# Four pairs as seven products in every gate-up group from the third on, and another order at the end of each group

## The chip, the cores and the metric

The kernel runs on one core of one Trainium2 chip. The metric is the device time of one execution in microseconds. Five engines work side by side, each with its own queue of instructions: PE (TensorE, matmuls; its weight loads are listed as PEld), DVE (VectorE), ACT (ScalarE), POOL (GpSimd) and SP (SyncE, which only issues DMAs here). They wait for each other through semaphores.

## What is computed

One layer of an encoder in float32, 256 tokens of width 2048: a feed-forward block (FFN), a mixer (a gated recurrence beside windowed attention), a second FFN. The change lies in the first half of each FFN, the gate-up product:

```
ff = swiglu(rms_norm(x, pre_norm_ffn1), w_ffn1_gate_up, w_ffn1_down)

def swiglu(x, w_gate_up, w_down):
    gate, up = jnp.split(x @ w_gate_up, 2, axis=-1)      # 2048 -> 2 x 5632
    return (jax.nn.silu(gate) * up) @ w_down
```

The result must have nearly float32 accuracy.

## The kernel before

**Three products for one.** TensorE multiplies numbers of a shortened float32 format (fp32r). Each operand is split into a high part and the rest: ACT casts the high part (L176, `scalar.copy`), DVE or POOL subtracts it from the original for the low part (L177, `tensor_tensor`). A product is then three matmuls: high times high, high times low, low times high (`three`, L438). All of them are issued at one line, L447, with 128 x 128 weights (activations) and 512 moving columns.

**Groups and pairs.** The 5632 gate and 5632 up columns are worked off in 11 groups (`NG`) of 512 gate and 512 up columns. Within a group the 2048 rows of the weight are 8 pairs (u = 0 to 7) of two blocks of 128 rows. One pair of one group is a tile `raw` of 128 x 2048: four blocks b11, b12, b22, b21 of 512 columns, 1 MB, fetched by two DMAs from SP (`fetch_tile`, L140). There are five such tiles; a tile is refilled (`load_next`, L970) as soon as its last split is issued. Four PSUM banks c[m][n] hold the sums, m a half of the tokens, n gate or up.

**Plain or seven.** A *plain* pair is 8 block products of three matmuls: 24. A pair done as a *seven* uses the 2 x 2 scheme with seven products: 21 matmuls. It needs sums of the weight blocks and sums of the activations, and four more banks p = P1, P5, P6, P7, which collect over all sevens of a group and are added into c once, at the group's end. The seven products of `products` (L473) are numbered 0 to 6: P1; into c00; into c01; P5; P7; P6; into c10. For a seven, `prepare` (L979) splits block b11 and has POOL issue a DMA that adds the neighbouring blocks in memory onto the tile (`add_second`, L146, 512 KB). `splits` (L994) then makes three splits of 1024 columns (called lower, upper and last) with two DVE additions of 512 columns between (L1001, L1002). A plain pair needs two splits of 1024 only. The splits go into rings of five high and five low tiles.

**Which pairs are sevens.** `MIXED_IN` is (2, 4, 5, 6), `FIVE` is (2, 3, 4, 5, 6). Group 1 has three sevens, group 2 four, groups 3 to 10 (`FIVE_IN`) five. Group 0 is done by other code. The fifth needs sums of activations for pair 3, which group 2 makes on the side (`sums_apart`, L1129), and one more room for a prepared block (`spare`, L1121).

**Order.** The loop at L1417 is written out by hand (`manual_schedule`), so each engine's instructions stand in program order. For each group 1 to 10: `first_pairs` (pairs 0 and 1, with the last steps of the group before between: its silu, gate times up, transposes, all in `units`, L1170); `pair_ahead` for pairs 2 to 5, which splits one pair ahead and prepares sevens further ahead; then, at L1421, the splits of pair 7 (a plain one, its low parts by POOL), the products of pair 6 (a seven, L1422), and `boundary` (L1252).

**The boundary** brings P1, P5, P6, P7 into the c banks and works pair 7 between. ACT copies P1 to SBUF (L1259). DVE then does eight additions: into c00 (L1260), a + P6 (L1261), + P7 (L1262), into c10 (L1263), a difference with P5 (L1266), into c01 (L1267), another (L1269), into c11 (L1270). Each that writes a bank must come before the matmuls of pair 7 into that bank. Pair 7's matmuls are parted by `take_parted` (L1015): `upper(m, n)` is the four with high weights for one bank, `lower()` the eight with low weights for all. The order on TensorE is upper of c00, c10, c01, c11, then lower. In pair 6 the order of products is 0, 1, 3, 4, 5, 6, 2.

Of the kernel before, what the change touches and what calls it, by code (L numbers as in the profile page):

```python
# [17 lines left out]
ALU = mybir.AluOpType  # L18
# [30 lines left out]
def hymba_layer_kernel(  # L49
# [19 lines left out]
    nc = tc.nc  # L69
# [145 lines left out]
    last = {}  # L215
# [186 lines left out]
    class Blocks:  # L402
# [4 lines left out]
        ahead = None  # L407
# [27 lines left out]
        def bank(self, at):  # L435
            return self.p[at[1]] if at[0] == "p" else self.c[at[1]][at[2]]
# [462 lines left out]
    NG = DFF // 512  # L899
# [5 lines left out]
    ADDED = 3  # L905
    FIVE = (2, 3, 4, 5, 6)
    PREPARED_FIVE = {2: -0.5, 3: 0.5, 4: 1.5, 5: 2.5, 6: 3.5}
    FIVE_IN = range(3, NG)
    AWAY = 8
    MIXED = range(0, 20, 2)  # L910
    MIXED_EARLY = MIXED[:8]
# [11 lines left out]
    class Gated(Blocks):  # L923
# [23 lines left out]
        def plan(self, opened=False):  # L947

            some = MIXED_IN[1:3] if opened else MIXED_IN[:3]
            self.here = {  # L950
                g: FIVE if g in FIVE_IN else MIXED_IN if g > 1 else some for g in range(1, NG)
            }
# [62 lines left out]
        def take_parted(self, g, u):  # L1015

            (h0, l0), (h1, l1) = self.split_of.pop((g, u))
            del self.raws[g, u]
            a = self.tiles[u]

            def parts(m, n, k):
                ms = slice(m * P, (m + 1) * P)
                o = (n ^ k) * 512
                cs = slice(o, o + 512)
                return ("c", m, n), a[:, k, 0, ms], a[:, k, 1, ms], (h0, h1)[k][:, cs], (l0, l1)[k][:, cs]

            def upper(m, n):
                for k in range(2):
                    at, ah, al, h, _ = parts(m, n, k)
                    self.some_of(at, (ah, h), (al, h))  # L1030

            def lower():
                for k in range(2):
                    for n in range(2):
                        for m in range(2):
                            at, ah, _, _, l = parts(m, n, k)
                            self.some_of(at, (ah, l))

            return upper, lower

        def take(self, g, u):

            got = self.split_of.pop((g, u))
            del self.raws[g, u]
            first = self.firsts.pop((g, u), None)
            if first:
                before_fold = u == KT // 2 - 2
                self.products(u, first, *got, (0, 1, 3, 4, 5, 6, 2) if before_fold else range(7))
                return ()
            hs, ls = zip(*got)  # L1050
            return [
                (lambda k=k, m=m, n=n: self.plain(u, hs, ls, m, n, k))
                for k in range(2)
                for m in range(2)
                for n in range(2)
            ]
# [27 lines left out]
    def ffn(gated, w_dn, post_gain, again, gain=None, lead=None, opening=None):  # L1084

        with ExitStack() as st:
# [136 lines left out]
            def some(steps, n):  # L1223
                for _ in range(n):
                    next(steps)

            last = KT // 2 - 1
# [24 lines left out]
            def boundary(g, ahead):  # L1252

                a, b = room_for("z"), room_for("s")
                c, (p1, p5, p6, p7) = gated.c, gated.p
                add = nc.vector.tensor_tensor
                bank, lower = gated.take_parted(g, last)

                nc.scalar.copy(a, p1)  # L1259
                add(c[0][0], c[0][0], a, ALU.add)  # L1260
                add(b, p6, a, ALU.add)  # L1261
                add(a, p7, b, ALU.add)  # L1262
                add(c[1][0], c[1][0], a, ALU.add)  # L1263
                bank(0, 0)
                bank(1, 0)
                add(b, p5, b, ALU.subtract)  # L1266
                add(c[0][1], c[0][1], b, ALU.add)  # L1267
                bank(0, 1)
                add(b, p5, a, ALU.subtract)  # L1269
                add(c[1][1], c[1][1], b, ALU.add)  # L1270
                bank(1, 1)
                lower()
                some(ahead, 2)

            def first_pairs(g, waiting, ahead):

                gated.group(g)
                sevens = FIVE if g in FIVE_IN else MIXED_IN
                if ahead:
                    some(waiting, 2)  # L1280
                    gated.prepare(g, sevens[1], nc.gpsimd)
                    some(ahead, 1)
                else:
                    some(waiting, 1)
                    gated.prepare(g, sevens[1])
                    some(waiting, 1)
                    ahead = gated.splits(g, 1)
                    some(ahead, 2)
                    gated.prepare(g, sevens[2])
                for one in gated.take(g, 0):  # L1290
                    one()
                some(waiting, 1)
                ahead = gated.splits(g, 2)
                some(ahead, 2)
                next(ahead, None)
                some(waiting, 1)
                for one in gated.take(g, 1):
                    one()

            def pair_ahead(g, u):  # L1300

                if u == 2 and g in FIVE_IN:
                    gated.prepare(g, FIVE[3])
                if u == 3:
                    gated.prepare(g, MIXED_IN[3])
                ahead = gated.splits(g, u + 1)
                some(ahead, 2)
                for one in gated.take(g, u):
                    one()
                if u == last - 2 and g < NG - 1:  # L1310
                    gated.prepare(g + 1, MIXED_IN[0])
                for _ in ahead:
                    pass
                if u == last - 2:
                    done = gated.split_of[g, last - 1][-1][1]
                    nc.gpsimd.tensor_copy(warm[:, 2:3], done[:, 0:1].bitcast(F32))
                if g == 1 and u in sums_at:
                    sums_in(sums_at[u])
                if g == 2 and u in (2, 3, 4):
                    if u == 2:  # L1320
                        apart.append(sums_apart(ADDED))
                    next(apart[0])
                if u == 5 and 1 < g <= AWAY // 2 + 1:
                    put_away(2 * g - 4)
                    put_away(2 * g - 3)
# [12 lines left out]
            raws, firsts, got = {}, {}, {}  # L1338
# [73 lines left out]
            with tc.manual_schedule():  # L1412
# [4 lines left out]
                for g in range(1, NG):  # L1417
                    first_pairs(g, waiting, begun)
                    for u in range(2, last - 1):
                        pair_ahead(g, u)  # L1420
                    some(gated.splits(g, last, nc.gpsimd), 2)  # L1421
                    for one in gated.take(g, last - 1):  # L1422
                        one()
                    boundary(g, gated.splits(g + 1, 0) if g < NG - 1 else splits(0))
                    if g < NG - 1:
                        begun = gated.splits(g + 1, 1)
                        next(begun)
                    among = None
                    if g < NG - 1:
                        third = (FIVE if g + 1 in FIVE_IN else MIXED_IN)[2]  # L1430
                        among = lambda g=g, u=third: gated.prepare(g + 1, u, nc.gpsimd)
                    waiting = units(gated.c, rest, among)
                    some(waiting, 2)
# [12 lines left out]
                ahead = splits(1)  # L1446
# [5 lines left out]
                ahead = splits(2)  # L1452
# [4 lines left out]
                for i in range(2, 2 * NU - Pairs.HELD):  # L1457
# [4 lines left out]
                    ahead = splits(i + 1)  # L1462
# [31 lines left out]
    gated = Gated(w_ffn1_gate_up, two_banks())  # L1494
    xt = new_xt()
    gated.see(xt)
    with tc.manual_schedule():
# [17 lines left out]
        first = gated.source(0)  # L1515

        def arrive(i, eng=nc.sync):
# [3 lines left out]
        h, l = (  # L1521
            p.tile([P, 1024], F32R, tag=t, name=nm(t)) for p, t in ((hip, "h"), (lop, "l"))
        )
# [12 lines left out]
        def parts(u, i, n=2):  # L1536

            if i == 0:
                gated.parts[u] = ([], [])
            h, l = (  # L1540
                p.tile([P, 1024], F32R, tag=t, name=nm(t)) for p, t in ((hip, "h"), (lop, "l"))
            )
            w = 1024 // n
            for j in range(n):
                split_act(
                    h[:, j * w : (j + 1) * w],
                    l[:, j * w : (j + 1) * w],
                    raws[u][:, i * 1024 + j * w : i * 1024 + (j + 1) * w],
                )
            for part, of in zip(gated.parts[u], (h, l)):  # L1550
                part.append(of)
# [173 lines left out]
    with ExitStack() as s2:  # L1725
# [142 lines left out]
        with tc.manual_schedule(engines=ordered):  # L1868
            late = [load(mix_tile("N", 6144, kc)) for kc in (2, 3)]
            parts = [split(late[0]), ([], [])]  # L1870
# [35 lines left out]
            bank = spread_begin(ratio, 1)  # L1906
            bounds_ahead()
            first = [split_half(raw, 0)]
# [50 lines left out]
            bank = spread_begin(rest)  # L1959
# [14 lines left out]
            g = mid.tile([P, 2, 512], F32, tag="g", name="g")  # L1974
# [73 lines left out]
        k = wide[:, 0].rearrange("p (d j t) -> p d j t", d=2, t=T)  # L2048
# [342 lines left out]
        g = gates(1)  # L2391
# [27 lines left out]
        gated = Gated(w_ffn2_gate_up, two_banks())  # L2419
# [139 lines left out]
```

## Time and profile before

| | us |
|---|---|
| median of 3 runs (1822.75 to 1824.27) | 1823.04 |
| the profiled execution | 1823.13 |
| its span, first to last instruction | 1821.4 |
| PE busy | 1798.4 |
| DVE busy | 1648.0 |
| ACT busy | 1143.9 |
| POOL busy | 288.5 |

The profile shows one execution. A row of a group of instructions has line, engine, operation, tiles (written <- read) with their shapes, count, then busy time and mean nanoseconds of one, then how long the engine was idle just before them and what ended that. A row of a timeline has start and length in microseconds. A row of the waits says who waited for whom: total, times, longest. PE's busy time is made of instructions that overlap. The first FFN's groups 1 to 10 lie from about 45 to 476 us of the span, the second's from about 1153 to 1587.

### The profile page before, as it was taken

The page shows a single profiled execution, that of the slowest core. Times are in us where ns is not written, and L with a number is a line of the kernel's source. Part 1 is how long each engine was busy: PE and PEld are TensorE (multiplying, and loading weights), DVE is VectorE, ACT ScalarE, POOL GpSimd, SP SyncE. Part 2 cuts the span into 40 slices and gives each one's busy share as a digit, 9 for nine tenths or more (in the row PEclk, how much of TensorE's full clock was granted, in tenths as well). Part 3 has the DMA queues.
Part 4 walks back from the last instruction along what each step waited for, and adds up shares of the span by engine and source line. Part 5 has one row for each costly group of instructions (what it writes and reads, how often), then busy time and mean ns, then how long its engine had stood idle before and what let it go on. Part 6 is the DMA issues. An engine that isn't in the chain of part 4 may idle for free.

```text
span 1821.4 us, 24095 instructions
## 1 busy us (share of the span) xinstructions
PE 1798.4 (99%) x8320; PEld 1480.1 (81%) x8320; DVE 1648.0 (90%) x2154; ACT 1143.9 (63%) x1527; POOL 288.5 (16%) x270
## 2 busy tenths in 40 slices
PE   9999999999999999999999999999999999999998
PEld 7877787777788888888899888877777778788886
DVE  6899999999999999888888888889999999999997
ACT  7556666666665667566667566556666656566663
POOL 0122322222110100000000000022223222200110
PEclk9999999999999999999999999999999999999999
DMA  9789999899799997954555767889999899799895
GB/s 369 231 246 283 284 296 261 262 256 253 237 325 306 310 281 244 295 160 165 181 166 173 254 206 262 249 236 270 285 278 279 255 270 260 199 319 340 270 318 167
DMA packets 130331, 469.05 MB, mean 258 GB/s; under 512 B 14608, under 2 KB 17424, under 8 KB 128672
## 3 DMA queue, kind: packets, MB, share of 16 engines
q1 hardware_dynamic: 109152, 391.18, 59.5%
q0 software_dynamic: 20912, 76.07, 23.5%
q8 instruction: 65, 1.06, 0.2%
q14 instruction: 58, 0.48, 0.1%
q10 hardware_dynamic: 144, 0.26, 0.0%
HBM read 452.77 MB, written 14.68 MB: 257 GB/s over the span
## 4 chain that ended last, share of the span: by engine, by line
PE 86%; DVE 9%; DMA 2%; ACT 1%; issue 1%; SPq 0%; POOL 0%; DVEq 0%; ACTq 0%; POOLq 0%
PE pa L447 39%; PE pb L447 34%; PE pa L315 6%; PE pa L320 3%; DVE l L177 1%; DMA raw<-in_w_ffn_gate_up_dram 1%; ACT h L176 1%; DVE pa L1267 1%; DVE pb L1270 1%; DVE s L1269 1%; DVE z L1262 1%; DVE pb L1263 1%; PE pa L369 1%; DVE s L1261 1%; PE pa L368 1%
## 5 line engine op out<-in xcount | busy, mean ns | idle before, releaser
L176 ACT CAST h<-raw 128x1024 fp32r<-128x1024 f32 (+1 forms) x881 | 850.6, 1002 | 428.2 <-DVE raw L1002 99.8
L177 DVE TENSOR_TENSOR l<-raw,h 128x1024 fp32r<-128x1024 f32 (+1 forms) x789 | 915.6, 1191 | 64.3 <-ACT h L176 45.5
L447 PE MATMUL pa<-h,xt 128*128 128x512 f32 x1214 | 407.9, 393 | 4.3 <-DVE pa L1267 3.9
L447 PE MATMUL pb<-h,xt 128*128 128x512 f32 x1012 | 350.9, 395 | 7.2 <-DVE pb L1270 5.4
L447 PEld LDWEIGHTS pa<-h,xt 128*128 128x128 f32 x1214 | 226.3, 188 | 59.0 <-DVE pa L1267 12.8
L447 PEld LDWEIGHTS pb<-h,xt 128*128 128x128 f32 x1012 | 186.8, 188 | 61.1 <-DVE pb L1270 14.1
L447 PE MATMUL pa<-l,xt 128*128 128x512 f32 x583 | 227.6, 390 | 0.4 <-DVE l L177 0.4
L447 PE MATMUL pb<-l,xt 128*128 128x512 f32 x506 | 197.1, 389 | 0.0
L177 POOL TENSOR_TENSOR l<-raw,h 128x1024 fp32r<-128x1024 f32 (+1 forms) x76 | 142.7, 1897 | 207.7 <-ACT h L176 202.4
L447 PE MATMUL pb<-h,ht 128*128 128x512 f32 x428 | 151.2, 389 | 0.0
L447 PE MATMUL pa<-h,ht 128*128 128x512 f32 x428 | 151.1, 389 | 0.0
L148 POOL DMA_DIRECT2D raw<-in_w_ffn_gate_up_dram x93 | 81.7, 890 | 420.1 <-DVE l L177 369.5
L447 PEld LDWEIGHTS pa<-l,xt 128*128 128x128 f32 x583 | 109.5, 188 | 23.4 <-DVE l L177 1.4
L447 PE MATMUL pa<-h,xs 128*128 128x512 f32 x328 | 117.5, 389 | 0.5 <-DVE sums L399 0.5
L447 PE MATMUL pb<-h,xs 128*128 128x512 f32 x328 | 114.3, 389 | 0.0
L447 PEld LDWEIGHTS pb<-l,xt 128*128 128x128 f32 x506 | 95.0, 188 | 19.8
L315 PE MATMUL pa<-xt,h 128*128 128x512 f32 x448 | 109.9, 393 | 0.0
L315 PEld LDWEIGHTS pa<-xt,h 128*128 128x128 f32 x448 | 81.5, 188 | 15.3
L447 PEld LDWEIGHTS pb<-h,ht 128*128 128x128 f32 x428 | 80.3, 188 | 16.6
L447 PEld LDWEIGHTS pa<-h,ht 128*128 128x128 f32 x428 | 80.3, 188 | 16.6
L148 POOL DMA_DIRECT2D raw<-in_w_ffn_down_dram x42 | 36.5, 868 | 348.0 <-DVE la L177 276.8
L447 PE MATMUL pa<-l,ht 128*128 128x512 f32 x214 | 83.3, 389 | 0.0
(345 smaller groups left out, 2681.5 us busy)
## 6 DMA issues: line engine op xcount, KB each, us to landing
raw<-in_w_ffn_gate_up_dram SPq DMA_DIRECT2D x350, 512.0 KB, 6.4
raw<-in_w_ffn_down_dram SPq DMA_DIRECT2D x176, 512.0 KB, 8.5
raw<-in_w_mix_in_dram SPq DMA_DIRECT2D x94, 512.0 KB, 4.8
raw<-in_w_ffn_gate_up_dram POOLq DMA_DIRECT2D x93, 512.0 KB, 8.9
raw<-in_w_ffn_down_dram POOLq DMA_DIRECT2D x42, 512.0 KB, 8.7
ht<-away SPq DMA_DIRECT2D x24, 512.0 KB, 10.5
raw<-in_w_mix_out_dram SPq DMA_DIRECT2D x24, 512.0 KB, 5.9
away<-ht SPq DMA_DIRECT2D x16, 512.0 KB, 9.2
```

The source lines that it names most:

```text
L148: nc.gpsimd.dma_start(raw[:, 0:1024], src[:, 512:1536], accum_op=ALU.add)
L176: nc.scalar.copy(hi, src)
L177: by.tensor_tensor(lo, src, hi.bitcast(F32), ALU.subtract)
L315: nc.tensor.matmul(slot[f], weights(hs, kk, f), xcol(xt, k), start=(k == 0), stop=(k == KT - 1))
L320: nc.tensor.matmul(slot[f][:, 0:T], weights(ls, kk, f), xcol(xt, kh * 8 + kk, 0), start=False, stop=False,)
L368: nc.tensor.matmul(dst, xh, l[:, o : o + n], start=False, stop=False)
L369: nc.tensor.matmul(dst, xl, h[:, o : o + n], start=False, stop=(k == KT - 1))
L447: nc.tensor.matmul(self.bank(at), lhs, rhs, start=(n == 1), stop=n in (ends, self.of[at]), skip_group_check=n > ends,)
L1261: add(b, p6, a, ALU.add)
L1262: add(a, p7, b, ALU.add)
L1263: add(c[1][0], c[1][0], a, ALU.add)
L1267: add(c[0][1], c[0][1], b, ALU.add)
```

## The change

`FIVE_IN` becomes empty: groups 3 to 10 now take `MIXED_IN`, four sevens (2, 4, 5, 6), like group 2, and pair 3 is plain. The job of `sums_apart` in group 2 and the extra room fall away with it.

The boundary is put in another order. In pair 6 the products go 0, 3, 4, 5, 1, 6, 2 (P1, P5, P7, P6, c00, c10, c01). The splits of pair 7 are issued behind pair 6's products and behind the copy of P1. On DVE a + P6 comes first, then the addition into c00, then as before. Pair 7's matmuls go bank by bank with the low ones of its first block row among them (`most`: 4 + 1), and three low ones of the second block row stand ahead of bank c11. All groups 1 to 10 get this. In `first_pairs` the second split of pair 1 is issued before the preparing of a seven, not behind it.

```
-    FIVE_IN = range(3, NG)
+    FIVE_IN = ()
...
-            def lower():
-                for k in range(2):
-                    for n in range(2):
-                        for m in range(2):
-                            at, ah, _, _, l = parts(m, n, k)
-                            self.some_of(at, (ah, l))
+            def lower(m, n, k):
+                at, ah, _, _, l = parts(m, n, k)
+                self.some_of(at, (ah, l))
...
-                self.products(u, first, *got, (0, 1, 3, 4, 5, 6, 2) if before_fold else range(7))
+                self.products(u, first, *got, (0, 3, 4, 5, 1, 6, 2) if before_fold else range(7))
...
-                bank, lower = gated.take_parted(g, last)
-
                 nc.scalar.copy(a, p1)
+                some(gated.splits(g, last, nc.gpsimd), 2)
+                upper, lower = gated.take_parted(g, last)
+
+                def most(m, n):
+                    upper(m, n)
+                    lower(m, n, 0)
+
+                add(b, p6, a, ALU.add)
                 add(c[0][0], c[0][0], a, ALU.add)
-                add(b, p6, a, ALU.add)
                 add(a, p7, b, ALU.add)
                 add(c[1][0], c[1][0], a, ALU.add)
-                bank(0, 0)
-                bank(1, 0)
+                most(0, 0)
+                most(1, 0)
                 add(b, p5, b, ALU.subtract)
                 add(c[0][1], c[0][1], b, ALU.add)
-                bank(0, 1)
+                most(0, 1)
                 add(b, p5, a, ALU.subtract)
                 add(c[1][1], c[1][1], b, ALU.add)
-                bank(1, 1)
-                lower()
+                for m, n in ((0, 0), (1, 0), (0, 1)):
+                    lower(m, n, 1)
+                most(1, 1)
+                lower(1, 1, 1)
                 some(ahead, 2)
...
                 if ahead:
                     some(waiting, 2)
+                    some(ahead, 1)
                     gated.prepare(g, sevens[1], nc.gpsimd)
-                    some(ahead, 1)
...
-                if g == 2 and u in (2, 3, 4):
+                if FIVE_IN and g == 2 and u in (2, 3, 4):
...
-                    some(gated.splits(g, last, nc.gpsimd), 2)
                     for one in gated.take(g, last - 1):
```

## The prediction

> **What bounds the kernel now.** I read the page first, then the sums over single groups, then the chain of waits, then the timelines of one group's end.
>
> ```profile
> PE 1798.4 (99%) x8320; PEld 1480.1 (81%) x8320; DVE 1648.0 (90%) x2154; ACT 1143.9 (63%) x1527; POOL 288.5 (16%) x270
> L447 PE MATMUL pa<-h,xt 128*128 128x512 f32 x1214 | 407.9, 393 | 4.3 <-DVE pa L1267 3.9
> L447 PE MATMUL pb<-h,xt 128*128 128x512 f32 x1012 | 350.9, 395 | 7.2 <-DVE pb L1270 5.4
> ```
>
> The matmul engine is busy nearly the whole span, so the change is costed on its path: matmuls added, stalls removed. The idle columns name two adds of the group's end (L1267, L1270) but only some 11 us. The next view, waits of the weight loads, gives the same adds and a third a larger figure:
>
> ```profile
> PEld pb L447 <- DVE pb L1270: 14.1, 20, 0.8
> PEld pa L447 <- DVE pa L1267: 12.8, 20, 1.0
> PEld pb L447 <- DVE pb L1263: 10.2, 20, 0.8
> 149.94 2.72 PE pa L447 x12
> ```
>
> Twenty waits each: one in each of the 20 groups that end in `boundary`. The last row is of the chain that ended last: twelve matmuls in 2.72 us, so one costs 0.2267 us when nothing waits. The busy time of one (393 ns) overlaps its neighbours, so stalls must be read from starts. The sums by group, cut at the starts of L1270:
>
> ```profile
> 91.30:134.38 43.08, 42.51 (x189) 34.34 (x188) 39.16 (x52) 26.24 (x34) 10.98 (x9) 1.00 0.83 237
> 134.38:176.81 42.43, 41.90 (x187) 33.83 (x186) 39.76 (x48) 26.74 (x32) 11.86 (x10) 1.00 0.94 275
> 176.81:219.20 42.39, 41.87 (x187) 33.82 (x186) 39.85 (x47) 26.92 (x32) 11.94 (x10) 1.00 0.95 282
> ```
>
> The first row is group 2, which has four pairs as sevens already; the others are groups 3 and 4, with five. So the trace of before shows four beside five at the old end of group. The columns are length, then busy time of PE, PEld, DVE, ACT, POOL, then granted clock (1.00), DMA share and GB/s. Group 2 is longer by 0.65 to 0.69, where three matmuls more (24 for a plain pair, 21 for a seven) make 3 x 0.2267 = 0.68. Vector work, DMA share and rate are lower in it. So a group's length is its matmuls plus something fixed, and neither DVE nor DMA sets it.
>
> The fixed part is at the end of the group. Group 2, TensorE:
>
> ```profile
> 126.41 0.39 PE L447 MATMUL pa<-h,xt 128*128 128x512 f32 x1
> 126.86 0.62 PE L447 MATMUL pa<-h,xt 128*128 128x512 f32 x2
> 129.58 0.39 PE L447 MATMUL pb<-h,xs 128*128 128x512 f32 x1
> 131.17 1.07 PE L447 MATMUL pa<-h,xt 128*128 128x512 f32 x4
> 132.28 1.20 PE L447 MATMUL pb<-h,xt 128*128 128x512 f32 x4
> 133.67 1.19 PE L447 MATMUL pa<-h,xt 128*128 128x512 f32 x4 [0.19 <-DVE pa L1267]
> 135.13 1.20 PE L447 MATMUL pb<-h,xt 128*128 128x512 f32 x4 [0.27 <-DVE pb L1270]
> 136.17 0.39 PE L447 MATMUL pa<-l,xt 128*128 128x512 f32 x1
> ```
>
> Pair 6, a seven, starts at 126.41; 129.58 is the last matmul of its fifth product, P6. Pair 7 starts at 131.17: four matmuls into each of four banks, then eight low ones. From 131.17 to 136.17 there are 16 matmuls, worth 3.63 us, in 5.00: 1.37 us of stall. The bracketed idle times show only 0.46 of it. DVE in the same stretch:
>
> ```profile
> 124.82 2.95 DVE L177 TENSOR_TENSOR l<-raw,h 128x1024 fp32r<-128x1024 f32 x3
> 128.48 0.70 DVE L1260 TENSOR_TENSOR pa<-pa,z 128x512 f32<-128x512 f32 x1 [0.70 <-ACT z L1259]
> 130.00 0.69 DVE L1261 TENSOR_TENSOR s<-pb,z 128x512 f32<-128x512 f32 x1 [0.83 <-PE pb L447]
> 130.73 0.69 DVE L1262 TENSOR_TENSOR z<-pb,s 128x512 f32<-128x512 f32 x1
> 131.53 0.70 DVE L1263 TENSOR_TENSOR pb<-pb,z 128x512 f32<-128x512 f32 x1
> 132.92 0.70 DVE L1267 TENSOR_TENSOR pa<-pa,s 128x512 f32<-128x512 f32 x1
> 134.38 0.70 DVE L1270 TENSOR_TENSOR pb<-pb,s 128x512 f32<-128x512 f32 x1
> ```
>
> It waits 0.83 for P6, then runs seven adds in series, (134.38 - 130.00) / 6 = 0.73 a step. The second, third and fourth bank are ready when L1263, L1267 and L1270 end; TensorE comes after 4, 8 and 12 matmuls, sooner than that each time.
>
> **The change, part by part.**
>
> *One pair fewer as seven, groups 3 to 10.* Eight groups in each of two FFNs, three matmuls more: 48 x 0.2267 = +10.9 us. They lie on the path, as the step of 0.68 shows. DVE, ACT, POOL and DMA have less to do, and so does group 2, which loses the job that made sums for the fifth pair; nothing waits for them there, so I cost that at nothing.
>
> *P6 one product earlier, c11 later.* Order 0, 3, 4, 5, 1, 6, 2 makes P6 the fourth product: its add can start 3 x 0.2267 = 0.68 earlier, at 129.32. But the add into c00 (L1260, 0.70), which ran before in DVE's wait, now comes behind it. So the add into c10 is the fourth of eight, 129.32 + 3 x 0.73 = 131.51, ending 132.21; that into c01 starts 132.97, ends 133.67; that into c11 starts 134.43, ends 135.13. Each lands within 0.05 of where it did. The chain isn't shorter; TensorE reaches each bank later.
>
> *The new order of pair 7.* Each bank now takes five matmuls before the next, and three low ones stand ahead of the last. From a release to the matmul is 0.05 (135.08 to 135.13), and the four matmuls after it took 1.04 instead of 0.91 (135.13 to 136.17): 0.13 for a restart. TensorE is at c10 at 131.17 + 5 x 0.2267 = 132.30, the release at 132.26. That is level; I charge the restart, 132.43. It is at c01 at 133.56, released 133.72: 0.16 + 0.13. It would be at c11 after eight more, 135.66; released 135.18, no wait. Sum 0.13 + 0.29 = 0.42 against 1.37: 0.95 saved. Bounds: with independent steps of 0.60 (L1263 to the next add, which starts under its tail) the chain is some 0.2 shorter, 0.2 of stall; with DVE 0.3 later it is 0.7. I take 0.42, as most steps depend on the one before.
>
> Over 20 groups: 20 x 0.95 = -19.0.
>
> *What is moved for it.* The copy of P1 goes ahead of pair 7's splits on ACT, and these behind pair 6's products in program order.
>
> ```profile
> 125.01 2.95 ACT L176 CAST h<-raw 128x1024 fp32r<-128x1024 f32 x3 [1.54 <-DVE raw L1002]
> 127.87 0.57 ACT L1259 COPY z<-pa 128x512 f32<-128x512 f32 x1
> 127.98 4.78 POOL L177 TENSOR_TENSOR l<-raw,h 128x1024 fp32r<-128x1024 f32 x2
> 168.18 2.95 DVE L177 TENSOR_TENSOR l<-raw,h 128x1024 fp32r<-128x1024 f32 x3
> 168.82 0.39 PE L447 MATMUL pa<-h,xt 128*128 128x512 f32 x1
> ```
>
> P1 ends at 126.86 + 0.62 less one 0.23, 127.25: the copy can stand at 127.3, then the two casts (the second and third of the three above) end near 128.9 and 129.9. TensorE wants them at 131.17 and 131.62. POOL's two low halves, 2.4 each, start near 128.9 and not at 127.98, done 131.3 and 133.7; they are wanted at the fifth matmul, 132.08, and near 135. Cover 0.8 and 1.3; if the first is used up, the lateness is paid in each group. POOL's queue order stays, and pair 7's reload on SP waits for POOL as before, some 0.9 later. In the next group's start a cast of 1.05 goes ahead of a prepared block's cast, so POOL and its 512 KB accumulating DMA come a microsecond later; that pair is split two pairs on (a pair is 4.8 us or more of matmuls), so nothing. `lower`, `upper` add no instruction.
>
> The fourth product needs pair 6's last low half 10 matmuls after the pair's start. In group 2 it is there at 127.77, wanted at 128.68: 0.9 early. In group 3, with five, 171.13 against 168.82 + 2.27 = 171.09: level. Four keeps that cover.
>
> *Weighed.* Rows: by the idle columns 11.5 us can be won at these adds (4.3 + 7.2), by the starts 20 x 1.37 = 27.4. The Trainium skill, "Perfetto Trace Analysis", Identifying Performance Opportunities, says matmul busy share is no good measure of the distance to roofline, and LDWEIGHTS busy share is; the same page says the profiler's end of a matmul is an estimate. By that the weight loads' waits (37.1 in three rows, 81% busy) are the ones to read, and the sum is mine; by the idle columns it would be the third rival below.
>
> **Sum.** +10.9 - 19.0 = -8.1. The profiled execution took 1823.13 (span 1821.4 and 1.7 around it), 0.09 above the median of the runs, 1823.04. 1823.1 - 8.1 = 1815.0.
>
> **Rivals.**
>
> *Slower: pair 6's low half comes late.* The place is the fourth product. If, with ends of group shorter, DVE no longer has its 0.9 there, P6 stalls by d, the chain of adds starts d later, and stall per group is about 0.42 + d + 0.13. It decides from a stall of 0.83 (saved 0.54, 20 x 0.54 = 10.9), so d = 0.28: low half at 128.68 + 0.28, 1.2 us later than group 2 has it. At d = 0.6 the group saves 0.22: -4.4 + 10.9 = +6.5, 1829.6. For it: group 3 has no cover at all. Against: DVE has a seven less. Chance 0.08.
>
> *The moved splits come late.* Allotted behind pair 6's products, their buffers could be those that pair 6 frees; its sixth product ends at 126.41 + 18 x 0.2267 + 0.16 = 130.65 (0.16: a matmul ends that long behind the start of the next), the cast after it at 131.7, and the weight load in front of the third matmul wants it near 131.4: 0.35 with the restart, 20 times, 7 us. 1822.0, no change. Against: the buffers of pair 5 are freed first. Chance 0.10.
>
> *The idle columns are right.* Then at most 11.5 x 0.95 / 1.37 = 8.0 is won against 10.9: 1826.0, no change. Against: 43.08 and 42.43 leave no room for it. Chance 0.04.
>
> **Numbers.** Forecast 0.78. Its own range: stall 0.25 to 0.65 a group gives -22.4 to -14.4, plus 10.9: 1811.6 to 1819.6. Some groups now lose 0.3 more than 1.37, which the lower end takes in: 1810.8. Towards the second rival up to 1821.2. A measurement tells about 0.2%, 3.6 us, from no change, so faster is below 1819.4: nearly all of the forecast, 0.77; same 0.15 (second and third rival and a rest); slower 0.08.
>
> **What would show it.** Right: L447 with 48 more matmuls; a middle group near 43.08 - 0.95 = 42.1 from c11 add to c11 add; DVE's wait for P6 gone 0.68 earlier and eight adds unbroken; TensorE's waits on the c10 add nearly nil, on the c01 add 0.2 to 0.3, on c11 none. Wrong: a wait on `l` of L177 at P6 or in pair 7 (first two rivals), a group over 42.4, or a wait moved into the next group's first pair, whose low half DVE now delivers only some 0.7 us ahead.

## The result and the profile after

The changed kernel took 1812.74 us (median of 4 runs, 1812.21 to 1813.40) against 1822.89 of the kernel before on the same chip (4 runs): 10.15 less, a ratio of 0.9944 with a 95% interval of 0.9926 to 0.9961. Forecast were 8.1 less and 1815.0. In two of the experiments below the execution that was profiled took two and nearly five times as long as the others (3685.87 and 8452.35 us); the times told are those of the others, and both kernels were run once more.

The page of the changed kernel, the rows that answer to the first three of before:

```profile
PE 1799.2 (99%) x8368; PEld 1491.3 (82%) x8368; DVE 1593.4 (88%) x2074; ACT 1127.0 (62%) x1487; POOL 278.0 (15%) x254
L447 PE MATMUL pa<-h,xt 128*128 128x512 f32 x1198 | 412.3, 393 | 0.1
L447 PE MATMUL pb<-h,xt 128*128 128x512 f32 x1044 | 360.5, 392 | 0.0
```

48 matmuls more (8368 for 8320), as costed. They are worth 10.9 us and the kernel is 10.15 shorter, so 21.0 us of stalls went. PE's busy time hardly moved, 1798.4 to 1799.2, though 10.9 us of matmuls came in: about half of those stalls had been inside that busy time. The idle columns fell from 11.5 to 0.1, which is the other half. The weight loads' waits on the adds:

```profile
PEld pa L447 <- DVE pa L1269: 7.3, 18, 0.4
PEld pb L447 <- DVE pb L1265: 4.5, 18, 0.3
```

Three rows with 37.1 us have become two with 11.8: c10 (L1265) and c01 (L1269). The wait on c11 is gone. 18 and not 20: group 1 waits no more. Groups 3 and 4, cut at the starts of the add into c11 (now L1272), one row each:

```profile
133.31:175.39 42.08, 42.08 (x190) 34.45 (x189) 36.70 (x43) 25.80 (x30) 11.20 (x9) 1.00 0.92 279
```
```profile
175.39:217.49 42.10, 42.10 (x190) 34.47 (x189) 36.70 (x43) 25.82 (x30) 11.25 (x9) 1.00 0.91 275
```

42.1 was forecast. DVE has 3.1 us a group less to do than with five (39.8). The end of group 3, TensorE:

```profile
167.41 0.39 PE L447 MATMUL pa<-h,xt 128*128 128x512 f32 x1
...
169.90 0.39 PE L447 MATMUL pb<-h,xs 128*128 128x512 f32 x1
...
172.17 1.07 PE L447 MATMUL pa<-h,xt 128*128 128x512 f32 x4
173.07 0.39 PE L447 MATMUL pa<-l,xt 128*128 128x512 f32 x1
173.30 1.19 PE L447 MATMUL pb<-h,xt 128*128 128x512 f32 x4
174.32 0.39 PE L447 MATMUL pb<-l,xt 128*128 128x512 f32 x1
174.69 1.20 PE L447 MATMUL pa<-h,xt 128*128 128x512 f32 x4
...
176.64 1.08 PE L447 MATMUL pb<-h,xt 128*128 128x512 f32 x4
...
178.01 0.39 PE L447 MATMUL pa<-h,xt 128*128 128x512 f32 x1
```

Pair 6 starts at 167.41, P6 ends its issue at 169.90, pair 7 takes 172.17 to 178.01: 5.84 for 24 matmuls worth 5.44, 0.40. Of this 0.34 are the two waits (c10: 174.32 - 173.30 = 1.02 for 0.91; c01: 174.69 - 174.32 = 0.37 for 0.23, and 0.11 in the next matmul), the rest is spread. DVE beside it:

```profile
165.21 2.96 DVE L177 TENSOR_TENSOR l<-raw,h 128x1024 fp32r<-128x1024 f32 x3
170.40 0.69 DVE L1262 TENSOR_TENSOR s<-pb,z 128x512 f32<-128x512 f32 x1 [2.23 <-PE pb L447]
171.01 0.70 DVE L1263 TENSOR_TENSOR pa<-pa,z 128x512 f32<-128x512 f32 x1
...
172.54 0.70 DVE L1265 TENSOR_TENSOR pb<-pb,z 128x512 f32<-128x512 f32 x1
...
173.93 0.70 DVE L1269 TENSOR_TENSOR pa<-pa,s 128x512 f32<-128x512 f32 x1
...
175.39 0.70 DVE L1272 TENSOR_TENSOR pb<-pb,s 128x512 f32<-128x512 f32 x1
```

From the start of pair 6 the adds into c10, c01, c11 start at 5.13, 6.52 and 7.98. In group 2 of before (pair 6 at 126.41) they started at 5.12, 6.51 and 7.97. DVE comes no sooner; TensorE comes later and has other work meanwhile. Pair 6's last low half ends at 168.17, wanted at 169.67: 1.5 ahead.

### The profile page after: what moved, and what is told of

It reads as the page before. It is cut to its first block, busy times and chain, and to the rows that moved or that the text cites. A ratio compares the mean times of both kernels' runs of the same rounds, so it can differ in the third digit from the quotient of the medians.

```text
span 1811.3 us, 23981 instructions
## 1 busy us (share of the span) xinstructions
PE 1799.2 (99%) x8368; PEld 1491.3 (82%) x8368; DVE 1593.4 (88%) x2074; ACT 1127.0 (62%) x1487; POOL 278.0 (15%) x254
## 4 chain that ended last, share of the span: by engine, by line
PE 91%; DVE 3%; DMA 2%; ACT 1%; issue 1%; SPq 0%; POOL 0%; DVEq 0%; ACTq 0%
PE pa L447 42%; PE pb L447 36%; PE pa L315 6%; PE pa L320 3%; DVE l L177 1%; DMA raw<-in_w_ffn_gate_up_dram 1%; DMA raw<-in_w_mix_in_dram 1%; PE pb L1858 1%; DMA X<-in_x_dram 1%; PE pa L1198 1%; PE pb L1198 1%; ACT h L176 1%; PE pa L369 0%; PE pa L368 0%; PE pa L367 0%
## 5 line engine op out<-in xcount | busy, mean ns | idle before, releaser
L176 ACT CAST h<-raw 128x1024 fp32r<-128x1024 f32 (+1 forms) x849 | 833.7, 1009 | 447.1 <-PE pb L447 144.8
L177 DVE TENSOR_TENSOR l<-raw,h 128x1024 fp32r<-128x1024 f32 (+1 forms) x773 | 896.8, 1187 | 100.3 <-ACT h L176 79.3
L447 PE MATMUL pa<-h,xt 128*128 128x512 f32 x1198 | 412.3, 393 | 0.1
L447 PE MATMUL pb<-h,xt 128*128 128x512 f32 x1044 | 360.5, 392 | 0.0
L447 PEld LDWEIGHTS pb<-h,xt 128*128 128x128 f32 x1044 | 194.6, 188 | 44.1 <-DVE pb L1265 4.5
L148 POOL DMA_DIRECT2D raw<-in_w_ffn_gate_up_dram x77 | 67.5, 877 | 417.8 <-DVE l L177 368.8
L447 PEld LDWEIGHTS pb<-l,xt 128*128 128x128 f32 x522 | 98.0, 188 | 20.3
```

What stands on the lines that cost most here:

```text
L148: nc.gpsimd.dma_start(raw[:, 0:1024], src[:, 512:1536], accum_op=ALU.add)
L176: nc.scalar.copy(hi, src)
L177: by.tensor_tensor(lo, src, hi.bitcast(F32), ALU.subtract)
L447: nc.tensor.matmul(self.bank(at), lhs, rhs, start=(n == 1), stop=n in (ends, self.of[at]), skip_group_check=n > ends,)
```

## The experiments

Two views were to be told apart. The *order theory* (the prediction's): a group is its matmuls plus a stall, the stall is how far DVE's adds land behind TensorE's coming to each bank, and the two parts of the change add up. The *relief theory*: the gain is that DVE, ACT and DMA have less to do with four. A third view puts it on the earlier P6 or the earlier copy of P1.

**Four, the old end of group.** The kernel before with `FIVE_IN = ()` alone.

> The kernel before with only the count changed: four pairs as sevens in groups 3 to 10, the old end of group kept. Order theory (a group is its matmuls plus the stall at its end, and the two parts of the change add up): 48 matmuls more at 0.2267 = +10.9, the stall of 1.33 to 1.37 a group stays: about 1833.5, groups of 43.08. Relief theory (the gain comes from DVE and DMA having less to do with four): the stall shrinks without the new order, the time is at or below 1823.

Measured 1833.06, ratio 1.0052 (1.0037 to 1.0067). Of the 10.9 of the count 9.8 are there (1823.26 for the kernel before in the same runs), so the relief gives about 1 us and no more. The trace shows where: four groups of the kernel before were 0.1 to 0.4 longer than the rest, and here groups 2 to 10 all have 43.05 to 43.10. DVE's busy time fell to 1601.1 us.

**Five, the new end.** The changed kernel with

```
+    FIVE_IN = range(3, NG)
```

> The changed kernel with five pairs as sevens in groups 3 to 10 again. Order theory: 10.9 less than the changed kernel, 1801.9, if pair 6's last low half is there for the fourth product; if that comes level with its use, as in the kernel before, 0.1 to 0.3 a group is lost in 16 groups, up to 1806.5. Relief theory: the new end does not work with five, stalls of a group stay near 1.3 and the time is above 1812, near 1820.

> Five with the new end once more, for a usable profile: 1804.6 again. The order theory lets 1801.9 come of the sum; what is above it (0.17 a group in 16 groups) should show in the trace as a wait of P6's second matmul for pair 6's last low half (L177); if it is a wait at c10 or c01 instead, DVE starts its chain late for another reason.

Measured 1802.7 to 1805.5 (the middle one 1803.76), ratio 0.9893 (0.9876 to 0.9909); again 1803.29, 0.9892 (0.9877 to 0.9907). The new end works with five too, and going from five to four costs 9.0 to 9.5 us there, of the 10.9. Part of the remainder is the wait that the first rival of the prediction describes. The waits of this kernel (second run):

```profile
PEld pb L447 <- DVE l L177: 4.0, 7, 1.0
PEld pa L447 <- DVE pa L1269: 7.5, 18, 0.8
PEld pb L447 <- DVE pb L1265: 4.8, 18, 0.6
```

Seven waits of a weight load into `pb` for a low half. One of them, of 1.0, lies at 778 us, outside the groups, and the changed kernel has it too; the other six, 3.0 us, stand at P6's second matmul in six groups, where the changed kernel has none. The two of the adds are nearly as in it.

**Old order of pair 6's products** in the changed kernel.

```
-(0, 3, 4, 5, 1, 6, 2) if before_fold
+(0, 1, 3, 4, 5, 6, 2) if before_fold
```

> The changed kernel with pair 6's products in the old order 0, 1, 3, 4, 5, 6, 2, so that P6 is the fifth product again; all else new. Order theory: the chain of eight adds starts 0.68 later; waits come at c00 (about 0.44), c10 (0.39) and c01 (0.27), 1.10 a group against 0.34: +0.76 x 18 = +13.7, about 1826.5. Rival (the order of pair 7's matmuls alone makes the gain): within 2 of 1812.7.

Measured 1825.78 (10 runs), ratio 1.0013 (1.0004 to 1.0022): 13 more than the changed kernel, as worked out. With c00's add in the chain, the chain must start earlier. The new wait stands where it was expected:

```profile
215.08 0.39 PE L447 MATMUL pa<-h,xs 128*128 128x512 f32 x1
215.66 1.17 PE L447 MATMUL pa<-h,xt 128*128 128x512 f32 x4 [0.19 <-DVE pa L1263]
```

Pair 7's first matmul comes 0.58 after the last of pair 6, not 0.23: c00's add (L1263) is late.

**Old order of pair 7's matmuls** in the changed kernel: `most` without its `lower`, then all eight low ones behind.

> The changed kernel with pair 7's matmuls in the old order: four high ones into each of the four banks, then the eight low ones; products of pair 6, the copy and the adds stay in the new order. Order theory: the adds land where they landed before the change, TensorE comes to each bank as early as before, so the old stall of about 1.3 is back: 18 groups x 0.96 = +17.3, about 1830. Rival (the earlier P6 and the earlier copy make the gain): within 3 of 1812.7.

Measured 1832.33, ratio 1.0050 (1.0033 to 1.0067): 19.6 more. By the starts of the matmuls the stall is back at 1.34 in 18 groups, and group 1, which has none in the changed kernel, has 0.69 in each FFN: 18 x 1.00 + 2 x 0.69 = 19.4, hence 2 more than expected.

**c00's add out of the chain.** The changed kernel with

```
-(0, 3, 4, 5, 1, 6, 2) if before_fold
+(0, 1, 3, 5, 4, 6, 2) if before_fold
...
-                add(b, p6, a, ALU.add)
                 add(c[0][0], c[0][0], a, ALU.add)
+                add(b, p6, a, ALU.add)
                 add(a, p7, b, ALU.add)
```

> The changed kernel with the add into c00 taken out of the chain again: pair 6's products in the order 0, 1, 3, 5, 4, 6, 2 (P1, c00, P5, P6, P7, c10, c01; P6 is still the fourth) and on DVE the add into c00 ahead of a + P6. Order theory: c00's add runs while DVE waits for P6, the chain behind P6 has seven adds, each bank is ready 0.7 earlier, before TensorE comes to it: stall 0 and not 0.34 in 18 groups, -6.2: about 1806.5. Rival (what is left at the end of a group is a restart that each wait costs, or DVE is simply full): within 2 of 1812.7.

> As the run before, with five pairs as sevens in groups 3 to 10. Order theory: 48 matmuls less, -10.9: 1795.7; a little more if pair 6's low half comes level with the fourth product, up to 1799. Relief theory: DVE, fuller with five, can't follow the shorter groups, and the time stays near 1804.6, that of five with the new end.

Four: 1806.05, ratio 0.9912 (0.9898 to 0.9927). Five: 1797.07, ratio 0.9858 (0.9841 to 0.9874), the shortest of all and 25.7 below the kernel before it was run with. Both are where the order theory put them. Group 3 of four:

```profile
171.82 1.07 PE L447 MATMUL pa<-h,xt 128*128 128x512 f32 x4
172.73 0.39 PE L447 MATMUL pa<-l,xt 128*128 128x512 f32 x1
172.96 1.07 PE L447 MATMUL pb<-h,xt 128*128 128x512 f32 x4
...
174.09 1.07 PE L447 MATMUL pa<-h,xt 128*128 128x512 f32 x4
...
177.26 0.39 PE L447 MATMUL pa<-h,xt 128*128 128x512 f32 x1
```

171.82 to 177.26 is 5.44 for 24 matmuls: no stall. With five, what is left above 1795.7 is again pair 6's low half. In one group:

```profile
291.84 0.39 PE L447 MATMUL pb<-h,xs 128*128 128x512 f32 x1
292.83 0.50 PE L447 MATMUL pb<-l,xs 128*128 128x512 f32 x1 [0.60 <-DVE l L177]
```

P6's second matmul comes 0.99 after its first. Its line among that kernel's waits has nine of them, one of which is again the one outside the groups:

```profile
PEld pb L447 <- DVE l L177: 4.9, 9, 1.0
```

**The late copy.** The changed kernel with pair 7's splits ahead of the copy of P1 again.

> The changed kernel with the copy of P1 behind pair 7's two casts on ACT again, all else new. Order theory: the copy then ends some 2 us later, still ahead of P6 in groups with a seven as pair 6, so nothing there; group 1, where pair 6 is plain and P6 is done long before, may lose up to 1.2, twice: 1812.7 to 1815. Rival (the copy's place is what starts the chain earlier): the stall of 0.7 or more a group is back, over 1822.

> The late copy once more, for a usable profile; three of its times lay at 1813.4 to 1816.5. Order theory: what is above 1812.7 is group 1, where pair 6 is plain: a stall of about 1.2 in each of its two occurrences, and 0.34 in the others as in the changed kernel. If the others have more than that, the copy holds the chain of adds there too.

Measured 1813.4 to 1816.5 (ratio 0.9957, 0.9940 to 0.9974), and again 1811.5 and 1813.5 (0.9942, 0.9922 to 0.9962). The second run's waits on the adds are 7.5 us in 19 and 4.7 in 19, as in the changed kernel plus one group's: with four, the copy's place is worth nothing that can be measured. Group 1 did not lose the 1.2 that was allowed for.

**Old order in the first pairs** (a seven prepared ahead of pair 1's second split).

> The changed kernel with the preparing of a seven ahead of pair 1's second split again in the first pairs of a group. Order theory: both have cover there, so 1812.7 within 1.5. Rival (the next group's first pair, whose low half comes only some 0.7 ahead, needs it): 0.3 or more a group, 1818 or more.

Measured 1811.99, ratio 0.9941 (0.9924 to 0.9957): with four the order is worth nothing, though DVE loses 1.1 us in each of 16 groups by it (last section).

**Only pair 7's order.** The kernel before, five, with nothing but this:

```
-                bank, lower = gated.take_parted(g, last)
+                upper, lower = gated.take_parted(g, last)
+                def bank(m, n):
+                    upper(m, n)
+                    lower(m, n, 0)
...
-                bank(1, 1)
-                lower()
+                for m, n in ((0, 0), (1, 0), (0, 1)):
+                    lower(m, n, 1)
+                bank(1, 1)
+                lower(1, 1, 1)
```

> The kernel before (five) with one thing changed: pair 7's matmuls in the new order (five into a bank before the next, three low ones ahead of c11). Pair 6's products, the copy and the adds on DVE stay as they were. Order theory: the adds land at the same times after pair 6's start in the kernel before and in the changed one (within 0.05), so this alone makes the whole gain of the new end: stall about 0.34 and not 1.37, 20 x 1.0, 1802 to 1804, level with five with the new end (1803.3, 1804.6). Rival (the earlier P6 or the copy is needed with it, as the run with the old products, 13 slower, could be read): 1812 or more.

Measured 1814.91 (1812.94 to 1818.47), ratio 0.9957 (0.9942 to 0.9972): a miss. 8 us are won, not 20. Group 4 of this run, with five, on DVE:

```profile
208.66 0.69 DVE L1002 TENSOR_TENSOR raw<-raw 128x512 f32<-128x512 f32 x1
209.27 2.95 DVE L177 TENSOR_TENSOR l<-raw,h 128x1024 fp32r<-128x1024 f32 x3
212.92 0.70 DVE L1261 TENSOR_TENSOR pa<-pa,z 128x512 f32<-128x512 f32 x1 [0.70 <-ACT z L1260]
213.53 0.68 DVE L1262 TENSOR_TENSOR s<-pb,z 128x512 f32<-128x512 f32 x1
...
218.50 4.62 DVE L177 TENSOR_TENSOR l<-raw,h 128x1024 fp32r<-128x1024 f32 x3
```

and on TensorE:

```profile
209.11 0.39 PE L447 MATMUL pa<-h,xt 128*128 128x512 f32 x1
...
212.28 0.50 PE L447 MATMUL pb<-l,xs 128*128 128x512 f32 x1
212.61 0.40 PE L447 MATMUL pb<-h,xs 128*128 128x512 f32 x1
...
215.12 0.39 PE L447 MATMUL pa<-l,xt 128*128 128x512 f32 x1
215.79 1.20 PE L447 MATMUL pb<-h,xt 128*128 128x512 f32 x4 [0.29 <-DVE pb L1264]
```

Pair 6 starts at 209.11, its last low half ends at 212.22, 3.11 later; in group 3 of the kernel before it was 2.31. So DVE has fallen back. It had worked without idle time since the end of group 3. Its rows there, first in this run, then in the second run of five with the new end:

```profile
175.69 0.70 DVE L1271 TENSOR_TENSOR pb<-pb,s 128x512 f32<-128x512 f32 x1
176.30 4.62 DVE L177 TENSOR_TENSOR l<-raw,h 128x1024 fp32r<-128x1024 f32 x3
```
```profile
174.49 0.70 DVE L1272 TENSOR_TENSOR pb<-pb,s 128x512 f32<-128x512 f32 x1
175.10 3.49 DVE L177 TENSOR_TENSOR l<-raw,h 128x1024 fp32r<-128x1024 f32 x3
...
206.95 2.95 DVE L177 TENSOR_TENSOR l<-raw,h 128x1024 fp32r<-128x1024 f32 x3
```

From the add into c11 to the end of pair 6's last low half DVE takes 212.22 - 175.69 = 36.53 here and 209.90 - 174.49 = 35.41 there. The difference of 1.12 is that of the first three splits (4.62 and 3.49), in which POOL holds DVE up (last section). P6's second matmul waits for the low half (212.28). P6 ends at 212.61 + 0.40 = 213.01, but its add starts at 213.53, behind c00's, and that waited 0.70 for the copy, which stands behind pair 7's casts on ACT:

```profile
209.46 2.95 ACT L176 CAST h<-raw 128x1024 fp32r<-128x1024 f32 x3 [1.54 <-DVE raw L1002]
212.32 0.57 ACT L1260 COPY z<-pa 128x512 f32<-128x512 f32 x1
```

These casts had waited for DVE (L1002), so the copy is late through DVE too. The add into c10 comes 0.4 late.

**Only pair 7's order, four.**

> As the run with only pair 7's order new, but with four pairs as sevens in groups 3 to 10 (the kernel before with the count and pair 7's order changed; products of pair 6, copy, adds on DVE and the first pairs' order old). In the run with five the stall was 0.34 in group 2, which has four, and 0.8 to 1.1 in groups with five, where the copy of P1 and pair 6's low half came late. If that is DVE and ACT being too full with five in a shorter group, four has none of it: stall 0.34 in all groups, 1833.1 - 20 = 1813, level with the changed kernel. If the earlier P6, the copy and c00's add behind it are needed with four as well, 1820 or more.

Measured 1812.32 (1811.93 to 1813.47), ratio 0.9940 (0.9924 to 0.9957): level with the changed kernel. With four, the order of pair 7's matmuls makes the whole gain by itself; with five the earlier copy, the earlier P6 and the order in the first pairs, taken together, are worth 11.6 more (1814.91 to 1803.29). No run with five tries them apart. The traces speak for the first pairs' order: in the run with only pair 7's order DVE was held up by POOL for 1.10 to 1.14 us in each of 18 groups, with five and the new end once in all, for 0.48. With four there is idle time to take this from, with five there was none in the stretch above. That this order carries most of the 11.6 is likely by this, but not shown.

## Why the prediction was right

*Bound.* Right. Length of a group: matmuls plus a stall. Four with the old end costs 9.8 (1833.06 against 1823.26 in the same runs), forecast 10.9; old end against new with four differ by 20.3 (1833.06 against 1812.74), forecast 19.0.

*The size of the stall.* The stall per group was put at 0.42 and is 0.34; restarts of 0.13 were charged at c10 and c01, and the wait on c10 costs 0.10. In 18 groups that is 1.4 us. And group 1, counted with 0.42 like the others, has no such wait in the changed kernel: its pair 6 is plain, so P6 is done a pair earlier. That is 0.8 more. The four groups that had been 0.1 to 0.4 longer than the rest are 42.1 like the others, which is 1.2 more. Against this, the 1.37 of before holds only 1.33 of waits, 0.8 less in 20 groups. Summed over all 20 groups, by the starts of pair 7's matmuls, the waits were 27.8 us and are 6.2: 21.6 went, 19.0 were forecast. Of the 21.6 the added matmuls take 10.9 and 10.15 show in the time; where the last half microsecond went is open.

*The chain isn't shorter, TensorE comes later.* Right, and more so than was said: four with only pair 7's order reaches 1812.32. That P6 one product earlier and c00's add behind it cancel is borne out by the run with the old products (+13) on one side and the run with c00 first (-6.7) on the other: the second shows that the addition needn't have been put into the chain.

*Cover of what was moved.* Right: the copy, the first pairs' order and POOL's low halves cost nothing. Pair 6's low half had 1.5 of cover, 0.9 was forecast.

*First rival.* With four it doesn't come. With five it does, as the prediction said of group 3, "level", and its price is small where the chain has been given room: 3.9 us of waits in eight groups, and 1.4 us of the time (1797.07 against 1795.7).

*Second and third rival.* No wait for a moved split is to be seen. The idle columns would have given 1826; the stalls taken away were 10.15 + 10.9 = 21.0 us, nearly twice the 11.5 that they showed. The Trainium skill, "Perfetto Trace Analysis", Identifying Performance Opportunities, says that matmul busy share is no good measure of how close a kernel is to roofline; the trace agrees: that share stood at 99% before and after.

*What the forecast did not see.* That a shorter group with five takes DVE's room away, and that a change of order alone can cost DVE a microsecond more a group. That neither DVE nor DMA sets a group's length, as the prediction reads the rows of before, no longer holds for DVE there. The relief of four, costed at nothing and worth about 1 us at the old end, is worth some 13.5 us where only pair 7's order is new: four, with 10.9 us more of matmuls, takes 2.6 less than five there (1812.32 and 1814.91).

## What to carry to other kernels

Read the size of a matmul engine's stalls from the starts of its instructions against their spacing when nothing waits, not from the idle time. The waits of the weight loads name the cause, but add up to more (37.1 us before, 27.8 by the starts). Where another engine's serial chain releases buffers one by one, first give the waiting engine other work in between, then take out of the chain what can run before it. Before a stage is made shorter, see which engine beside it has just enough room now: what its load is worth depends on the length that is left.

## What the runs showed of the hardware

A DVE split (both inputs in SBUF) and a POOL split (both inputs in SBUF) shut each other out. In the run with only pair 7's order POOL worked a block of 512 columns, and DVE's third split began 0.03 after it:

```profile
220.73 1.30 POOL L177 TENSOR_TENSOR l<-raw,h 128x512 fp32r<-128x512 f32 x1 [3.51 <-ACT h L176]
220.76 2.35 DVE L177 TENSOR_TENSOR l<-raw,h 128x1024 fp32r<-128x1024 f32 x1
```

That split took 2.35, and DVE's three from 218.50 took 4.62 together. The same three took 3.49 in the run with four and c00 first, where POOL's block came only as they ended (178.45):

```profile
175.04 3.49 DVE L177 TENSOR_TENSOR l<-raw,h 128x1024 fp32r<-128x1024 f32 x3
```

So 1.1 us of DVE's time went in a group. Where POOL starts second it is POOL that waits: in the changed kernel its block takes 1.47 and not 1.30 when it begins 0.32 before DVE's three splits end (176.00 + 3.49 = 179.49):

```profile
179.17 1.47 POOL L177 TENSOR_TENSOR l<-raw,h 128x512 fp32r<-128x512 f32 x1 [4.49 <-ACT h L176]
```

The boundary's adds, one input in PSUM, keep their 0.68 to 0.70 in the changed kernel while POOL runs its 4.78 us beside them. The Trainium skill, "SBUF — State Buffer", Who interferes with whom, states this: a DVE instruction with two SBUF inputs contends with a GpSimd instruction that reads SBUF, the second to start waiting for the first to end, and one with at most one SBUF input does not. The trace agrees on both.

The first pairs' order bears on whether the two meet. The run that has the old one, and is otherwise the changed kernel, shows

```profile
175.94 4.60 DVE L177 TENSOR_TENSOR l<-raw,h 128x1024 fp32r<-128x1024 f32 x3
178.16 1.29 POOL L177 TENSOR_TENSOR l<-raw,h 128x512 fp32r<-128x512 f32 x1 [3.54 <-ACT h L176]
```

With four this costs nothing (1811.99). The order alone doesn't decide it: at a later split DVE loses 0.78 in 18 groups of the run with the old order of pair 7's matmuls, where the first pairs' order is new, and 0.25 to 0.27 in the kernel before, where it is old.
